# Low parts of streamed weights: a ScalarE negation and an adding DMA in place of a VectorE subtraction

## The chip, the cores and the metric

The kernel runs on one core of one Trainium2 chip. The metric is device time in microseconds (us) for one execution. A core has five engines with instruction queues of their own, each worked off in order: TensorE (PE in the profile, its weight loads PEld), VectorE (DVE), ScalarE (ACT), GpSimd (POOL) and SyncE (SP). DMAs are issued from the queues of SP, ACT and POOL, and 16 DMA engines move the data.

## The reference, cut to what matters

Two encoder layers on a sequence of 512 tokens of width 1024, all in float32. Nearly all the work is products of activations with weights that lie in device memory:

```
for l in range(DEPTH):                       # DEPTH = 2
    xn = rmsnorm(x, norm1_g[l])
    h = xn @ w_in[l]                         # projections of four token mixers
    ...                                      # the mixers a, b, c, d
    branch = jnp.einsum('bsnw,nwd->bsnd', ys, w_branch[l])
    gate = jax.nn.sigmoid(jnp.einsum('bsd,dne->bsne', xn, w_gate[l]))
    x = x + jnp.sum(gate * branch, axis=2) @ w_out[l]
    xn = rmsnorm(x, norm2_g[l])
    x = x + jnp.square(jax.nn.relu(xn @ w_mlp1[l])) @ w_mlp2[l]
return rmsnorm(x, final_norm_g)
```

## The kernel before

**High and low parts.** A product of float32 precision is made of three products of a rounded type (fp32r): each operand is cut into a high part (the value rounded to fp32r) and a low part (value minus high part), and TensorE adds high x high, high x low and low x high in PSUM. A weight block `raw` becomes `wh` (ScalarE, line 288, a cast) and `wl` (VectorE, line 289, `raw - wh`).

**Loads.** All products with weights stand in one list of items, the dense stream, and each item names its loads. A load is 512 KB: four blocks of 128 rows by 256 columns (`wl_a`; 512 runs of 1 KB in memory) or eight blocks by 128 columns (`wl_b`; 1024 runs of 512 B); in the chip's memory it is a tile of 128 partitions by 1024 elements. 276 loads come straight from a weight tensor and carry the key `"ap"` (40 of them `wl_b`). Two loads (`small`) are put together by several DMAs (`"custom"`). 98 loads (`"src"`) belong to the first MLP product: blocks `wq`, most of them sums and differences made by GpSimd at line 808. The change is in the 276.

**What a load goes through.** `emit_dma` (line 271) has SP load `raw` into tile `wr`, which has two buffers. `emit_split` makes `wh` and `wl` in `G['sp']` = 2 halves of 128x512 elements. Both tiles have three buffers, so the split of load i can begin only when TensorE has finished with load i - 3. (The last four loads of the second MLP product of each layer have buffers of their own, `twh` and `twl`.) TensorE then uses `wh` and `wl` in turns from its first matmuls on (lines 388 to 390, 402 to 404, 431 to 433).

**Order.** `Item.get(k)` is called when TensorE's matmuls of load i are about to be written down. It writes down the splits of all loads up to i + la, where `la` is 2 in the MLP and 1 elsewhere, then the preparing sums (`emit_pre`) and the DMAs up to i + 5. The mixers are generators. `drive` lets them run a step and then lets the dense stream run for so many estimated ns (`G`), so that dense matmuls stand between the steps of a mixer. The framework's scheduler may move an instruction ahead of another on the same engine, and it puts in all waits.

**Stages of a layer.** First come the norm and a front of projections and gates without a mixer beside them, then mixers a, d, b and c with projections, gates and branch products between their steps, then gates, branch products and `w_out` alone, the norm, and the MLP. In the MLP seven products `prod` of the first matrix (24 matmuls of 256 columns for each load) and four loads of the second (48 such matmuls each) take turns, seven times a layer; a last part (`tail_item`) closes it. After `prod` 6 the first load of the second matrix follows; this turn, from `m1` to `m2`, occurs 14 times in all.

Of the kernel before, what the change touches and what calls it, by code (L numbers as in the profile page):

```python
# [13 lines left out]
AF = mybir.ActivationFunctionType  # L14
ALU = mybir.AluOpType
AX = mybir.AxisListType

P = 128
# [14 lines left out]
G = dict(inv=1600, scan=1500, c=950, ss=300, kv=800, dr=1000, ds=1500, dh=1000, b1=900, b2=1100, b3=700, pd=8, ce=1100, hl=0, yp=4, pr=0, ps=0, b4=500, yn=1300, yw=1500, yt=1600, cl=3, sp=2, la=2, bl=(3, 5, 8), co=2500)  # L33
# [75 lines left out]
def encoder(ctx: ExitStack, tc: tile.TileContext, a: dict, out: bass.AP, dbg: dict = None):  # L109
    nc = tc.nc  # L110
    dbg = dbg or {}
    pe, dve, act, pool = nc.tensor, nc.vector, nc.scalar, nc.gpsimd
# [4 lines left out]
    sp = ctx.enter_context(tc.tile_pool(name="sp", bufs=8))  # L117
# [7 lines left out]
    def nm(s):  # L125
        cnt[0] += 1
        return f"{s}_{cnt[0]}"
# [23 lines left out]
    def f(ap):  # L151
        return ap.bitcast(F32)
# [80 lines left out]
    class Item:  # L233
# [6 lines left out]
        def get(self, k):  # L240
            i = self.i0 + k
            last = len(loads) - 1
            la = G['la'] if self.label[:2] in ("m1", "m2") else 1
            while ns_[0] <= min(i + la, last):
                stage(np_, ns_[0], emit_pre)
                emit_split(ns_[0])
                ns_[0] += 1
            stage(np_, min(i + 2 + la, last), emit_pre)
            stage(nd, min(i + 5, last), emit_dma)
            return wt.pop(i)  # L250

    def stage(ptr, upto, fn):
        while ptr[0] <= upto:
            if fn is emit_pre:
                stage(nd, ptr[0], emit_dma)
            fn(ptr[0])
            ptr[0] += 1
# [20 lines left out]
    def emit_split(i):  # L278
        w = loads[i]
        raw = w["src"]() if "src" in w else raws.pop(i)  # L280
        if "dest" in w:
            wh, wl = w["dest"]()
        else:
            wh = wp.tile([P, w["kt"], w["nc"]], F32R, tag="wh", name=nm("wh"))
            wl = wp.tile([P, w["kt"], w["nc"]], F32R, tag="wl", name=nm("wl"))
        n = w["kt"] // G["sp"]
        for k in range(0, w["kt"], n):
            act.copy(wh[:, k:k + n], raw[:, k:k + n])  # L288
            dve.tensor_tensor(wl[:, k:k + n], raw[:, k:k + n], f(wh[:, k:k + n]), op=ALU.subtract)  # L289
        wt[i] = (wh, wl)  # L290

# [1442 lines left out]
```

## Time and profile before

| | us |
|---|---|
| runs | 2342.53, 2341.07, 2341.0 |
| median | 2341.07 |
| the profiled execution, its own time | 2341.32 |
| its span, first to last instruction | 2339.3 |

The profile is of one execution. The 2.0 us between its span and its time lie around the instructions. A busy share is an average over all stages. What a change in one stage is worth is read from that stage and from the engine whose work ends last there. Matmuls are pipelined, so that the time of one (0.28 us for 256 columns) is longer than the step from one to the next.

### The profile page before, as it was taken

What the parts mean: (1) busy time and instruction counts of PE and PEld (TensorE: products, weight loads), DVE (VectorE), ACT (ScalarE), POOL (GpSimd) and SP (SyncE); (2) the same over time, 40 slices, a digit from 0 to 9 for tenths busy, and PEclk for the clock granted to TensorE, in tenths of its full rate; (3) what the DMA queues carried; (4) which work ended last, traced back from release to release, by engine and by line L of the source; (5) the groups of instructions that cost most, each with busy time, mean ns of one, the idle gap of its engine ahead of it and who ended that gap; (6) DMA issues with size and microseconds to landing.
All of it is one profiled execution on the core that took longest, in us unless ns stands there. A gap on an engine that the chain in (4) does not pass through costs nothing. (4 is left out here: it accounts for less than half of the span.)

```text
span 2339.3 us, 41459 instructions
## 1 busy us (share of the span) xinstructions
PE 2265.6 (97%) x16040; PEld 2027.1 (87%) x16040; DVE 1600.2 (68%) x2944; ACT 1236.9 (53%) x2827; POOL 749.8 (32%) x803
## 2 busy tenths in 40 slices
PE   7999999999999999999999999999999999999998
PEld 6879987878788989999987899878877889899998
DVE  5874547697886477677767745487877854867775
ACT  4565454765764264443445654367576633534443
POOL 1145452032332034443201545412313310434341
PEclk9999999999999999999999999999999999999999
DMA  6322131222122423233323111311322234233322
GB/s 153 99 46 64 50 92 59 64 91 82 51 71 82 162 71 123 87 109 109 111 75 91 55 55 60 96 54 55 100 73 64 64 115 137 88 95 109 100 82 91
DMA packets 234628, 200.80 MB, mean 86 GB/s; under 512 B 31680, under 2 KB 223552, under 8 KB 234432
## 3 DMA queue, kind: packets, MB, share of 16 engines
q1 hardware_dynamic: 231408, 193.08, 27.5%
q10 hardware_dynamic: 2304, 4.20, 0.5%
q8 instruction: 126, 2.06, 0.4%
q0 software_dynamic: 720, 0.89, 0.2%
q14 instruction: 70, 0.57, 0.1%
HBM read 190.24 MB, written 8.39 MB: 85 GB/s over the span
## 5 line engine op out<-in xcount | busy, mean ns | idle before, releaser
L289 DVE TENSOR_TENSOR wl<-wr,wh 128x512 fp32r<-128x512 f32 x540 | 405.3, 770 | 171.0 <-ACT wh L288 165.1
L288 ACT CAST wh<-wr 128x512 fp32r<-128x512 f32 x540 | 317.1, 621 | 220.4 <-PE pd L432 81.9
L431 PE MATMUL pd<-xh,wh 128*128 128x512 f32 (+1 forms) x768 | 309.1, 403 | 0.5 <-ACT xh L218 0.5
L432 PE MATMUL pd<-xl,wh 128*128 128x512 f32 (+1 forms) x768 | 298.4, 389 | 1.8 <-DVE xl L219 1.8
L433 PE MATMUL pd<-xh,wl 128*128 128x512 f32 (+1 forms) x768 | 298.4, 389 | 0.0
L389 PE MATMUL pd<-wl,hh 128*128 128x256 f32 x896 | 248.5, 277 | 0.0
L388 PE MATMUL pd<-wh,hh 128*128 128x256 f32 x896 | 248.0, 277 | 0.0
L390 PE MATMUL pd<-wh,hl 128*128 128x256 f32 x896 | 247.9, 277 | 0.0
L288 ACT CAST wh<-wq 128x512 fp32r<-128x512 f32 x196 | 115.2, 619 | 219.3 <-PE pd L390 92.8
L289 DVE TENSOR_TENSOR wl<-wq,wh 128x512 fp32r<-128x512 f32 x196 | 182.1, 963 | 13.3 <-ACT wh L288 13.2
L808 POOL TENSOR_TENSOR wq<-wq,wq 128x512 f32<-128x512 f32 x84 | 124.5, 1490 | 161.8 <-DVE wl L289 152.5
L433 PEld LDWEIGHTS pd<-xh,wl 128*128 128x128 f32 x768 | 146.0, 190 | 30.5
L432 PEld LDWEIGHTS pd<-xl,wh 128*128 128x128 f32 x768 | 146.7, 191 | 26.0 <-DVE xl L219 2.8
L388 PEld LDWEIGHTS pd<-wh,hh 128*128 128x128 f32 x896 | 168.2, 188 | 0.0
L390 PEld LDWEIGHTS pd<-wh,hl 128*128 128x128 f32 x896 | 168.2, 188 | 0.0
L389 PEld LDWEIGHTS pd<-wl,hh 128*128 128x128 f32 x896 | 168.1, 188 | 0.0
L431 PEld LDWEIGHTS pd<-xh,wh 128*128 128x128 f32 x768 | 146.2, 191 | 23.6 <-ACT xh L218 1.0
L676 DVE TENSOR_TENSOR x<-pd,x 128x512 f32<-128x512 f32 x124 | 85.2, 689 | 100.5 <-PE pd L390 100.4
L388 PE MATMUL pd<-wh,xh 128*128 128x256 f32 x512 | 151.0, 295 | 0.0
L389 PE MATMUL pd<-wl,xh 128*128 128x256 f32 x512 | 145.4, 284 | 0.0
L390 PE MATMUL pd<-wh,xl 128*128 128x256 f32 x512 | 145.0, 283 | 0.0
L1006 POOL TENSOR_TENSOR r<-r,r 128x512 f32<-128x512 f32 x26 | 36.5, 1402 | 300.7 <-PE pd L433 123.9
(393 smaller groups left out, 6631.6 us busy)
## 6 DMA issues: line engine op xcount, KB each, us to landing
wr<-in_w_in SPq DMA_DIRECT2D x92, 512.0 KB
wr<-in_w_mlp SPq DMA_DIRECT2D x72, 512.0 KB
wr<-in_w_gate SPq DMA_DIRECT2D x64, 512.0 KB
wq<-in_w_mlp SPq DMA_DIRECT2D x56, 512.0 KB
wr<-in_w_branch SPq DMA_DIRECT2D x32, 512.0 KB
wr<-in_w_out SPq DMA_DIRECT2D x16, 512.0 KB
x<-in_x SPq DMA_DIRECT2D x16, 256.0 KB
gsd<-gs ACTq DMA_DIRECT2D x16, 256.0 KB
```

What stands on the lines that cost most here:

```text
L288: act.copy(wh[:, k:k + n], raw[:, k:k + n])
L289: dve.tensor_tensor(wl[:, k:k + n], raw[:, k:k + n], f(wh[:, k:k + n]), op=ALU.subtract)
L388: mm(o, th, wh[:, k4, :], start=(kt == 0 and tt % 2 == 0), stop=False)
L389: mm(o, th, wl[:, k4, :], start=False, stop=False)
L390: mm(o, tl, wh[:, k4, :], start=False, stop=(kt == kts - 1 and tt % 2 == 1))
L431: mm(o, w1_, xh[kt][:, sl], start=(kt == 0 and hi_ == 0), stop=False)
L432: mm(o, w1_, xl[kt][:, sl], start=False, stop=False)
L433: mm(o, w2_, xh[kt][:, sl], start=False, stop=last)
L676: dve.tensor_tensor(d, bank.rearrange("p (t c) -> p t c", t=2), d, op=ALU.add)
L808: pool.tensor_tensor(d[:, k:k + 2], x[:, k:k + 2], y[:, k:k + 2], op=op)
L1006: pool.tensor_tensor(t, t, sh, op=ALU.add)
```

## The change

For loads with `"ap"` the cast is made in one piece. ScalarE then writes the negated high part into `wl`, and GpSimd issues a DMA that reads the weight block from memory a second time and adds it to `wl`. VectorE's subtraction is gone for these loads. `la` is 2 everywhere, and the memory set aside for descriptors of GpSimd's DMAs is doubled.

```diff
@@ -240,7 +240,7 @@
         def get(self, k):
             i = self.i0 + k
             last = len(loads) - 1
-            la = G['la'] if self.label[:2] in ("m1", "m2") else 1
+            la = G['la']
             while ns_[0] <= min(i + la, last):
@@ -283,9 +283,13 @@
-        n = w["kt"] // G["sp"]
+        n = w["kt"] // (1 if "ap" in w else G["sp"])
         for k in range(0, w["kt"], n):
             act.copy(wh[:, k:k + n], raw[:, k:k + n])
+            if "ap" in w:
+                act.activation(wl[:, k:k + n], f(wh[:, k:k + n]), AF.Copy, scale=-1.0)
+                pool.dma_start(wl[:, k:k + n], w["ap"].rearrange("(k p) c -> p k c", p=P)[:, k:k + n], accum_op=ALU.add)
+                continue
             dve.tensor_tensor(wl[:, k:k + n], raw[:, k:k + n], f(wh[:, k:k + n]), op=ALU.subtract)
         wt[i] = (wh, wl)
@@ -1719,7 +1723,7 @@
-    nc = bacc.Bacc("TRN2", target_bir_lowering=False, num_devices=1, dynamic_dma_scratch_size=4096)
+    nc = bacc.Bacc("TRN2", target_bir_lowering=False, num_devices=1, dynamic_dma_scratch_size=8192)
```

## Rows read from the trace of the kernel before

**Rows 1.** The page: span, and busy time of each engine.
```profile
span 2339.3 us, 41459 instructions
...
PE 2265.6 (97%) x16040; PEld 2027.1 (87%) x16040; DVE 1600.2 (68%) x2944; ACT 1236.9 (53%) x2827; POOL 749.8 (32%) x803
```

**Rows 2.** Stretches: us, busy PE, PEld, DVE, ACT, POOL, clock, DMA share, GB/s.
```profile
117.00:367.00 250.00, 245.11 (x2192) 214.63 (x2191) 137.02 (x226) 127.71 (x322) 120.93 (x150) 0.99 0.23 64
...
575.00:715.00 140.00, 133.65 (x677) 108.45 (x676) 115.62 (x358) 102.02 (x298) 45.30 (x49) 1.00 0.22 67
715.00:823.00 108.00, 108.00 (x642) 94.47 (x641) 51.75 (x94) 38.60 (x84) 15.64 (x13) 1.00 0.40 126
...
882.00:1148.00 266.00, 266.00 (x2306) 266.00 (x2305) 195.73 (x261) 117.22 (x207) 104.29 (x80) 1.00 0.33 101
```

**Rows 3.** Waits of PE: waited for, us in total, times, longest.
```profile
PE pm L483 <- DVE nj L468: 15.9, 9, 8.8
...
PE pm L833 <- DVE wl L289: 5.7, 2, 2.9
```

**Rows 4.** Timeline, turn from m1 to m2: cast, then TensorE's first matmul of that load.
```profile
2156.75 1.14 ACT L288 CAST wh<-wr 128x512 fp32r<-128x512 f32 x2 [1.63 <-PE pm L832]
...
2162.35 0.28 PE L388 MATMUL pd<-wh,hh 128*128 128x256 f32 x1
```

**Rows 5.** Timeline, gates alone: cast, then the first matmul of that load.
```profile
757.38 1.15 ACT L288 CAST wh<-wr 128x512 fp32r<-128x512 f32 x2 [1.62 <-PE pd L432]
...
768.54 0.39 PE L431 MATMUL pd<-xh,wh 128*128 128x512 f32 x1
```

**Rows 6.** Timeline, beside mixer a: cast, then the first matmul of that load.
```profile
249.20 1.23 ACT L288 CAST wh<-wr 128x512 fp32r<-128x512 f32 x2
...
271.98 0.28 PE L388 MATMUL pd<-wh,xh 128*128 128x256 f32 x1
```

**Rows 7.** Timeline, start of the MLP: cast of its second load, its first matmul.
```profile
831.54 1.14 ACT L288 CAST wh<-wr 128x512 fp32r<-128x512 f32 x2
...
835.96 0.28 PE L780 MATMUL pd<-xh,wh 128*128 128x256 f32 x1
```

**Rows 8.** Groups by line: busy us, mean ns | idle before, releasers.
```profile
L289 DVE TENSOR_TENSOR wl<-wr,wh 128x512 fp32r<-128x512 f32 x540 | 405.3, 770 | 171.0 <-ACT wh L288 165.1 <-PE pm L1152 4.3 <-PE pm L1614 0.2
L288 ACT CAST wh<-wr 128x512 fp32r<-128x512 f32 x540 | 317.1, 621 | 220.4 <-PE pd L432 81.9 <-PE pd L390 40.7 <-PE pm L832 22.0
...
L218 ACT CAST pth<-pm 128x128 fp32r<-128x128 f32 x160 | 40.8, 259 | 33.9 <-DVE ptl L219 24.5 <-PE pm L1604 9.4
```

**Rows 9.** Timeline: a 512 KB load issued by SP, the cast that waited for it.
```profile
2165.16 0.37 SPq L271 DMA_DIRECT2D wr<-in_w_mlp  x1
...
2168.65 1.15 ACT L288 CAST wh<-wr 128x512 fp32r<-128x512 f32 x2 [0.69 <-DMA wr<-in_w_mlp]
```

**Rows 10.** DMAs issued by POOL: size, us from issue to landing.
```profile
c_sgn<-in_sgn POOLq DMA_DIRECT2D x1, 448.0 KB, 7.0
c_negr<-in_neg POOLq DMA_DIRECT2D x1, 320.0 KB, 3.7
...
c_identr<-in_ident POOLq DMA_DIRECT2D x1, 64.0 KB, 3.7
...
c_identh<-in_ident POOLq DMA_DIRECT2D x1, 32.0 KB, 3.2
```

**Rows 11.** Timeline of POOL: one of these issues, 128 runs.
```profile
21.37 0.54 POOL L196 DMA_DIRECT2D c_negr<-in_neg  x1
```

**Rows 12.** SP's DMA queue: packets, MB, share of 16 engines.
```profile
q1 hardware_dynamic: 231408, 193.08, 27.5%
```

**Rows 13.** Stretches as in rows 2: a gap of PE, the stretch behind it, another gap.
```profile
863.70:866.70 3.00, 0.10 (x2) 0.03 (x1) 2.19 (x3) 1.38 (x3) 1.77 (x2) 1.00 0.00 0
867.27:870.68 3.41, 3.41 (x19) 3.41 (x18) 3.41 (x5) 0.00 (x0) 2.17 (x2) 0.50 0.00 0
...
628.00:629.90 1.90, 0.11 (x2) 0.04 (x1) 1.84 (x9) 1.13 (x4) 1.02 (x1) 1.00 0.20 62
```

## The prediction

> **What bounds the kernel now.** I read the busy shares first. TensorE is busy for 2265.6 of 2339.3 us, VectorE for 68%, ScalarE 53%, GpSimd 32% [rows 1]. Then the stretches: where no mixer runs, TensorE has no gap at all, in the gates and `w_out` (715 to 823) and in the MLP (882 to 1148); beside the mixers it loses 5 to 6 us in 250 or 140 us [rows 2]. So TensorE's order of work is the time, and a change of another engine counts only where it makes TensorE wait or ends a wait. TensorE's waits give what could be won: the longest is for the norm on VectorE (15.9 us), and the subtraction that the change touches appears with 5.7 us, both times for a `wq` block, which is not changed [rows 1, 3]. All idle time is 2339.3 - 2265.6 = 73.7 us.
>
> The next question is how early a load is ready, since the change lengthens its way. A cast begins when TensorE frees the third buffer (the releaser in the row). From the start of the cast to TensorE's first matmul of that load I find 5.60 us at the turn from `m1` to `m2` [rows 4], 11.16 us in gates alone [rows 5], 22.8 us beside mixer a [rows 6], and 4.4 us for the second load of the MLP [rows 7]. The first two are two loads' worth of matmuls, short at the turn because a `prod` has half as many. `la` = 2 can't lengthen them: three buffers set them, and the cast already starts when the buffer comes free.
>
> **Removed.** Two subtractions of 0.770 us for each of 276 loads [rows 8]: VectorE loses 425 us. They are done before TensorE needs them everywhere, so this alone gives nothing on TensorE's path except where a mixer's or norm's own VectorE step comes sooner. Of the 73.7 us idle I take 20 us as reachable in this way; bounds 0 and 25 us, a third of it.
>
> **Added on ScalarE.** A cast of 128x512 takes 621 ns and one of 128x128 259 ns [rows 8], 0.943 ns a column, so one of 128x1024 takes 621 + 512 x 0.943 = 1.10 us; the negation the same. A load costs ScalarE 2.21 us where it cost 1.24, in all +267 us, 53% to 64%. In the busiest mixer stretch, 575 to 715, with some 16 loads (one in 9 us), ScalarE goes from 73% to about 84%, VectorE from 83% to about 65%. What stands behind the negation on ScalarE, evacuations and mixer steps, waits 1 us more. I let this and the gain on VectorE cancel to +10 us, bounds -25 to +60.
>
> **Added on GpSimd and the DMA engines.** 276 issues and 276 x 512 KB. No row shows an adding DMA. Nearest below: a POOL DMA of 64 or 320 KB lands 3.7 us after its issue [rows 10]. Nearest above: one of 448 KB, which reads twice that and converts, behind four others, took 7.0 us [rows 10]. SP's 512 KB load took 3.5 us [rows 9]; the adding one has three streams in place of two and starts like a POOL DMA. A 512 KB load costs 27.5% x 2339.3 / (193.08 / 0.524) = 1.75 us of all 16 engines [rows 12]; a second read adds about that. I take 6.3 us from issue to landing, nearer to the 448 KB row, and keep 3.7 and 10. The issue itself is 0.54 us on POOL for 128 runs [rows 11]; a weight load has 512 or 1024. If each run costs, it is 2.2 or 4.3 us; I take 1 us inside the 6.3.
>
> The Trainium skill speaks here against the change: by "Collectives: The Full Stack" (The bandwidth ceiling) an add in the DMA path isn't dear itself but needs two source reads, which halved the measured rate. No run here shows it yet. By it the share of the DMA engines for an added load is 3.5 us, by a plain copy 1.75 us.
>
> **The way of a load, new:** cast 1.10 + negation 1.10 + hand-overs 0.2 + 6.3 = 8.7 us.
>
> - At the turn from `m1` to `m2`: 8.7 - 5.6 = 3.1 us late, 14 times, 43 us. The three loads behind it begin 2.8 to 5.4 us apart and TensorE spends 5.44 us on each (48 matmuls), so they are not late again as long as the way is under 10.9 us.
> - The clock: after a TensorE gap of 2.9 us the granted clock is 0.50, the level of 1.2 GHz, for 3.41 us; after one of 1.8 us it stays at 1.00 [rows 13]. Six such stretches are in the trace, each after a gap of 2.6 us or more. Each costs half its length, 1.7 us; 14 of them 24 us.
> - Second load of the MLP: 8.7 - 4.4 + 1.7 = 6 us, twice, 12 us.
> - Gates, `w_out` and the fronts alone, about 70 loads at 5.55 us: the way of 8.7 fits into 11.16. But the DMA engines, 0.40 busy there [rows 2], get 3.5 us more in each 5.55 us: 1.03. That is the limit; I take 0.3 us a load, 20 us (0 if the add costs a copy's share, 0.72).
> - Beside the mixers 8.7 us fit into 22.8 [rows 6], with a load about every 9 us at the least into some 16. POOL is 48% busy in 117 to 367 [rows 2], and an issue may stand behind a sum of 1.4 us that waits for the mixer; behind the issue wait the mixer's own sums. Nothing taken beyond the +10.
>
> Sum: 43 + 24 + 12 + 20 + 10 = 109 us. Against the profiled execution's own 2341.3 us, 0.25 us over the median, that is 2450 us. Ends: landing at 3.7 gives a way of 6.1 us, 7 us at the turns, 3 at the second load, -25 to 0 beside the mixers, 2326 to 2351; landing at 10 gives 12.4 us, so (6.8 + 1.7) x 14 = 119, 19 at the second loads, 70 x 0.65 = 46 where two loads' matmuls no longer cover it, 60 beside the mixers, 2585.
>
> **Rivals.**
>
> *Hidden, and VectorE's relief pays.* If the adding DMA lands within 3.2 us, as the 32 KB one did [rows 10], the way is 5.6 us and no turn is late; the relief of 20 us is left, 2321 us. The point is a landing of 3.2 us. Against it: 64 KB already took 3.7. By the Trainium skill, "DMA: Bandwidth & Descriptors" (Anatomy of one DMA), a POOL DMA takes about 2.0 us plus its bytes at 436 GB/s, an estimate of 3.2 us for 512 KB. The 64 KB row at 3.7 us is above that. 8%, and 12% that the landing is between this and 5 us (2346 to 2400 us).
>
> *The DMA engines become the bound.* If the add costs three copies' share, 5.25 us, gates and `w_out` want 2.2 + 5.25 = 7.5 us a load for 5.55 us of matmuls: 1.9 x 70 = 137 us. In the MLP, 0.33 + 4 x 5.25 / 41.6 = 0.83, the landings stretch to some 9.6 us and the way to 12: 113 us at the turns. With 20 at the other places, 2611 us. For it: the share of 1.03 above. 17%.
>
> *POOL writes each run.* 2.16 us for each of 236 loads and 4.3 us for 40: POOL +683 us, to 61%, in 117 to 367 to about 75%. The way becomes 10.3 us (12.5 for the 40): turns 90, second loads 20, 24 loads of the fronts at +0.65 16, gates 20, mixers' own sums delayed 40; 2527 us. 13%.
>
> *The change doesn't reach what bounds.* 98 of 376 loads keep their subtraction, and `la` acts on nothing that the buffers don't set; that is in the sum.
>
> **How the numbers follow.** A measurement tells about 0.2%, 5 us. Forecast near 2450 us (2400 to 2500): 50%. The range takes in the small landing, POOL's rival and the DMA bound and leaves out about 8% below and 10% above: 2350 to 2640 us. Faster 7% (the first rival, less a little), within 0.2% 5% (a landing near 3.7 with relief and stalls alike), slower 88%.
>
> **What would show it.** In the profile after: VectorE near 1180 us, ScalarE near 1500; TensorE waiting at line 388 or 389 for a POOL DMA of `wl` at each of 14 turns, 3 us, with a stretch at clock 0.50 behind it; no such waits beside the mixers; the DMA share near 1 in the gates. The adding DMA's row gives issue to landing: 6.3 right, 4 or 10 wrong by the terms above. Waits of TensorE for `wl` in the mixers, or mixer sums on POOL waiting for the issue, would make POOL's rival right.

## The result and the profile after

The changed kernel takes 2570.3 us (median of 4 runs, 2565.6 to 2573.6) against 2341.2 us in the runs beside it: ratio 1.098, 95% interval 1.096 to 1.099. It is slower, in the range that was given, but by 229 us where 109 were forecast. The profiled execution took 2565.6 us; its span is 224.5 us longer than that of [rows 1].

The page after: span and busy time by engine, the two DMA queues that carry the load, the median landings of the adding DMAs, and issues of them on GpSimd.

```profile
span 2563.8 us, 41353 instructions
...
PE 2325.7 (91%) x16040; PEld 2072.9 (81%) x16040; DVE 1263.2 (49%) x2392; ACT 1471.8 (57%) x2827; POOL 1076.9 (42%) x1079
...
q0 software_dynamic: 166928, 145.61, 39.2%
q1 hardware_dynamic: 231408, 193.08, 25.5%
...
L291 POOL DMA_DIRECT2D wl<-in_w_in x92 | 129.9, 1412 | 307.5 <-ACT wl L290 220.2
...
wl<-in_w_in POOLq DMA_DIRECT2D x92, 512.0 KB, 6.2
...
wl<-in_w_gate POOLq DMA_DIRECT2D x64, 512.0 KB, 6.1
```

VectorE is down by 337 us, ScalarE up by 235, GpSimd up by 327. TensorE has the same 16040 matmuls and is busy for 60 us more, since a part of them now runs at the low clock; the other 164 us are waits. GpSimd's queue q0 on the page before:

```profile
q0 software_dynamic: 720, 0.89, 0.2%
```

From 0.2% it went to 39.2%: (39.2% - 0.2%) x 2563.8 / 276 = 3.6 us of all 16 engines for each adding load.

Where TensorE waits now (waits of PE: waited for, us in total, times, longest):

```profile
PE pd L393 <- DMA wl<-in_w_mlp: 87.3, 16, 7.7
PE pm L487 <- DVE nj L472: 21.8, 7, 8.4
PE pd L408 <- DMA wl<-in_w_in: 15.2, 6, 5.8
PE pm L1371 <- DVE vb L1362: 10.9, 10, 2.8
```

The first line stands where [rows 3] had nothing: the low-part matmul of an `m2` load waits for its adding DMA, 14 turns and two more places. The second is the old wait for the norm.

The stretches of the first layer (columns as in [rows 2]; the same work as there, found by TensorE's loads): mixer a, mixer b's end, gates and `w_out`, MLP.

```profile
130.00:387.00 257.00, 243.51 (x2156) 212.25 (x2155) 106.15 (x170) 154.22 (x333) 146.78 (x191) 0.99 0.63 119
614.00:755.00 141.00, 135.03 (x684) 111.01 (x683) 98.56 (x319) 110.54 (x290) 62.21 (x64) 0.99 0.62 124
755.00:866.00 111.00, 107.08 (x609) 91.56 (x607) 24.13 (x55) 55.28 (x84) 36.70 (x31) 0.98 0.93 205
918.00:1262.00 344.00, 299.90 (x2431) 297.76 (x2430) 167.95 (x218) 151.66 (x227) 156.00 (x121) 0.93 0.55 125
```

The gates and `w_out` are where the DMA engines are fullest (0.93), and TensorE has lost only 3.9 us there. The MLP has a DMA share of 0.55 on the mean and has lost 44 us of TensorE's time to gaps, at a mean clock of 0.93.

To place the loss I took, for each of the 376 loads, the start of TensorE's first matmul of it after and before, and the growth of the difference over each part of the program. Later tables use the same parts, both layers together, in us. The border between the fronts and the mixers is soft: one load more or less moves 3 us. The start of the MLP begins here with the last load of `w_out`.

```
                       forecast   measured
turns m1 to m2, MLP          67      122.7
start of the MLP             12       23.3
fronts                       20       32.7
gates and w_out     (in the 20)       10.5
mixers                       10       35.4
sum                         109      224.6
```

One turn, seen closely (timeline of the fourth group in layer 0: ScalarE, GpSimd and TensorE):

```profile
1088.18 1.05 ACT L288 CAST wh<-wr 128x1024 fp32r<-128x1024 f32 x1 [1.64 <-PE pm L836]
1089.01 3.01 POOL L812 TENSOR_TENSOR wq<-wq,wq 128x512 f32<-128x512 f32 x2
1090.23 0.63 ACT L848 ACTIVATE c<-c 128x512 f32<-128x512 f32 x1 [1.00 <-DVE c L853]
1090.77 1.05 ACT L290 ACTIVATE wl<-wh 128x1024 fp32r<-128x1024 f32 x1
1092.17 1.31 POOL L291 DMA_DIRECT2D wl<-in_w_mlp  x1 [0.16 <-issue]
...
1093.78 0.63 PE L392 MATMUL pd<-wh,hh 128*128 128x256 f32 x4
...
1095.10 1.30 POOL L291 DMA_DIRECT2D wl<-in_w_mlp  x1 [0.55 <-ACT wl L290]
...
1098.03 1.30 POOL L291 DMA_DIRECT2D wl<-in_w_mlp  x1 [0.55 <-ACT wl L290]
...
1100.24 0.58 PE L393 MATMUL pd<-wl,hh 128*128 128x256 f32 x1 [5.84 <-DMA wl<-in_w_mlp]
```

TensorE reaches the load 5.60 us after its cast began, exactly the lead of [rows 4]. The negation begins 2.59 us after the cast, not 1.1: the square's relu stands between them and waits for VectorE. GpSimd finishes its two sums of `wq` only at 1092.02 and issues at 1092.17, 3.99 us after the cast. The DMA lands after 8.03 us. Over the 14 turns the medians are 3.99 us to the issue, 7.64 us to the landing, 11.63 us in all, against 8.7 in the forecast. The stretches of the same turn, same columns:

```profile
1094.41:1100.24 5.83, 0.00 (x0) 0.00 (x0) 1.99 (x3) 3.78 (x6) 4.73 (x5) 0.68 1.13 208
1100.24:1103.20 2.96, 2.96 (x14) 2.96 (x15) 0.00 (x0) 0.00 (x0) 0.17 (x1) 0.50 1.17 242
```

TensorE stands for 5.83 us, the granted clock falls to 0.50, its lower level, during the gap, and 14 matmuls after it run at that level. The DMA share is 1.13 to 1.17 (it adds up the packets' times, so it can pass 1): the second and third adding DMA, issued 2.9 us apart, run beside the first one.

### The profile page after: what moved, and what is told of

Its sections match the earlier page's. It is cut to its first block, busy times and chain, and to the rows that moved or that the text cites. A ratio compares the mean times of both kernels' runs of the same rounds, so it can differ in the third digit from the quotient of the medians.

```text
span 2563.8 us, 41353 instructions
## 1 busy us (share of the span) xinstructions
PE 2325.7 (91%) x16040; PEld 2072.9 (81%) x16040; DVE 1263.2 (49%) x2392; ACT 1471.8 (57%) x2827; POOL 1076.9 (42%) x1079
## 3 DMA queue, kind: packets, MB, share of 16 engines
q0 software_dynamic: 166928, 145.61, 39.2%
q1 hardware_dynamic: 231408, 193.08, 25.5%
## 4 chain that ended last, share of the span: by engine, by line
PE 55%; DMA 11%; ACT 11%; DVE 8%; POOL 7%; issue 6%; SPq 1%; POOLq 0%; DVEq 0%; ACTq 0%
PE pd L393 6%; PE pd L394 6%; PE pd L392 6%; DMA wl<-in_w_mlp 5%; PE pd L435 5%; PE pd L437 5%; PE pd L436 5%; ACT wh L288 2%; PE pd L408 2%; PE pd L406 2%; PE pd L407 2%; DMA wl<-in_w_in 2%; POOL wq L812 2%; PE pm L836 1%; PE pm L835 1%
## 5 line engine op out<-in xcount | busy, mean ns | idle before, releaser
L288 ACT CAST wh<-wr 128x1024 fp32r<-128x1024 f32 (+1 forms) x272 | 283.8, 1044 | 339.6 <-PE pd L394 162.9
L393 PE MATMUL pd<-wl,hh 128*128 128x256 f32 x896 | 263.2, 296 | 87.3 <-DMA wl<-in_w_mlp 87.3
L290 ACT ACTIVATE wl<-wh 128x1024 fp32r<-128x1024 f32 x268 | 283.9, 1059 | 4.0
L394 PE MATMUL pd<-wh,hl 128*128 128x256 f32 x896 | 259.7, 292 | 0.0
L291 POOL DMA_DIRECT2D wl<-in_w_in x92 | 129.9, 1412 | 307.5 <-ACT wl L290 220.2
L392 PE MATMUL pd<-wh,hh 128*128 128x256 f32 x896 | 254.1, 290 | 2.6 <-ACT wh L288 2.6
L393 PEld LDWEIGHTS pd<-wl,hh 128*128 128x128 f32 x896 | 182.5, 204 | 90.6 <-DMA wl<-in_w_mlp 90.5
L394 PEld LDWEIGHTS pd<-wh,hl 128*128 128x128 f32 x896 | 182.4, 204 | 0.0
L392 PEld LDWEIGHTS pd<-wh,hh 128*128 128x128 f32 x896 | 178.5, 202 | 3.0 <-ACT wh L288 3.0
L291 POOL DMA_DIRECT2D wl<-in_w_gate x64 | 83.2, 1300 | 223.1 <-ACT wl L290 177.0
```

The costliest lines, as they stand in the source:

```text
L290: act.activation(wl[:, k:k + n], f(wh[:, k:k + n]), AF.Copy, scale=-1.0)
L291: pool.dma_start(wl[:, k:k + n], w["ap"].rearrange("(k p) c -> p k c", p=P)[:, k:k + n], accum_op=ALU.add)
L392: mm(o, th, wh[:, k4, :], start=(kt == 0 and tt % 2 == 0), stop=False)
L393: mm(o, th, wl[:, k4, :], start=False, stop=False)
L394: mm(o, tl, wh[:, k4, :], start=False, stop=(kt == kts - 1 and tt % 2 == 1))
```

## The experiments

The theory after the result: a load costs what its way (cast, negation, issue, landing) exceeds its lead (cast to TensorE's first matmul), plus the low clock behind the gap; at the turns the landing is long because three adding DMAs run together. Rivals: the look-ahead or ScalarE's new work; GpSimd's place in the chain; a fixed cost per load through the engines.

**What is not the cause: look-ahead, ScalarE, VectorE.**

```diff
 # e1_la_only: the kernel before with
-            la = G['la'] if self.label[:2] in ("m1", "m2") else 1
+            la = G['la']
 # e8_no_add: the changed kernel without
-                pool.dma_start(wl[:, k:k + n], ..., accum_op=ALU.add)
```

> The kernel before with only the look-ahead of 2 for every load; the subtraction stays on VectorE. Theory (the way of an adding load is what costs): three buffers already set when a cast can begin, so 2341 us within 5. Rival (the earlier casts and subtractions stand ahead of the mixers' own steps, and this is the mixers' part of the loss): 2360 to 2380 us.

> The changed kernel without the 276 adding DMAs: the low part stays the negated high part, so the product of the low part is left out in what it means, not in its work. ScalarE's negation and the look-ahead stay. Theory (the landing is the late part of the way): the way at the turns falls from 11.6 to 3.6 us, under the lead of 5.6, no turn is late, and VectorE's relief shows: 2320 to 2345 us. Rival (ScalarE's extra 292 us is what delays the mixers): the mixers' 40 us stay, 2370 to 2390 us.

Measured: look-ahead alone 2352.0 us, ratio 1.005 (1.004 to 1.007); without the adding DMAs 2346.0 us, 1.002 (1.001 to 1.003). The look-ahead costs 11 us, against both expectations: more than my 5, less than the rival's 20; by parts 9.6 us of it are in the mixers. With the negation on ScalarE as well and 382 us less on VectorE (1217.9 us busy) the time is 6 us below that; what each of the two is worth was not separated. All but some 6 us of the loss comes with the DMA.

**GpSimd in the chain.** Three kernels put something else in the adding DMA's place.

```diff
 # in place of pool.dma_start(wl[:, k:k + n], ..., accum_op=ALU.add)
 # e14_pool_touch
+                pool.tensor_tensor(wl[:, k, 0:2], f(wl[:, k, 0:2]), raw[:, k, 0:2], op=ALU.add)
 # e16_pool_busy
+                pool.tensor_tensor(wl[:, 0:2], f(wl[:, 0:2]), raw[:, 0:2], op=ALU.add)
 # e11_small_add
+                pool.dma_start(wl[:, 0, 0:64], w["ap"][0:P, 0:64], accum_op=ALU.add)
```

> The changed kernel with each adding DMA cut from 512 KB to 32 KB: the low part is right in 64 columns of one of its four blocks alone, the rest stays the negated high part. What waits for what stays, the bytes go. Theory (half of a landing and more is the transfer, 3.6 us of all 16 engines): landing at 4 to 4.5 us, the way at the turns 3.6 + 4.3 = 7.9, late by 2.3 us, mostly without a fall of the clock: 14 x 2.3 = 32, 5 to 15 elsewhere over the 2346 us without the DMA: 2375 to 2395 us. Rival (GpSimd's place in the chain costs by itself: its sums stand behind an issue that waits for the negation): the mixers' 30 us stay, 2400 to 2440 us.

> The changed kernel with each adding DMA replaced by a sum of two columns on GpSimd that reads and writes the low part, so the rest of the low part stays the negated high part: GpSimd still waits in its order for ScalarE's negation, and TensorE for GpSimd, but nothing is issued and nothing has to land. The run with 32 KB DMAs kept 34 to 37 us of loss in the two mixer stretches though it landed in 2.6 us. Theory (that loss is GpSimd's order: the mixers' own sums stand behind an instruction that waits for the negation): the mixers' 30 to 37 us stay and the turns are on time, 2372 to 2385 us. Rival (it is the DMA itself, its issue of 0.9 us and its landing): 2345 to 2356 us, as without the DMA.

> The changed kernel with each adding DMA replaced by a sum of 512 columns on GpSimd, 1.3 us, as long as the issue of the adding DMA; so the second half of the low part stays the negated high part. No DMA. Theory (the mixers lose by GpSimd's time for the issue): the mixers lose 20 to 35 us over the 2349 us of the run with a sum of two columns, 2368 to 2385 us. Rival (it is the DMA that slows them, by the engines or by what its issue does to VectorE): 2346 to 2356 us.

Measured: 2424.2 us with 32 KB, ratio 1.035 (1.033 to 1.036); 2348.7 us with a sum of two columns, 1.003; 2393.5 us with a sum of 512 columns, 1.023 (1.021 to 1.024). By parts:

```
                     changed  32 KB  512 columns  2 columns
turns, MLP             122.7   30.5          3.9        2.4
start of the MLP        23.3    7.6          0.8        0.3
fronts                  32.7    7.8         14.6        2.0
gates and w_out         10.5    2.4          3.1        1.0
mixers                  35.4   37.4         29.5        2.1
```

The GpSimd lines of the three: first the issue of 32 KB (duration ns min/median/max) and its landing in us, then the two sums (busy us, mean ns | idle before).

```profile
L291 POOL DMA_DIRECT2D wl<-in_w_in x92: 849/876/1134, 38.9 to 1804.8; - x92
...
wl<-in_w_in POOLq DMA_DIRECT2D x92, 32.0 KB, 2.6
```
```profile
L291 POOL TENSOR_TENSOR wl<-wl,wr 128x512 fp32r<-128x512 f32 (+1 forms) x268 | 332.6, 1241 | 711.2 <-ACT wl L290 586.1 <-issue 86.2 <-ACT dn L1455 15.9
```
```profile
L291 POOL TENSOR_TENSOR wl<-wl,wr 128x2 fp32r<-128x2 f32 x268 | 60.6, 226 | 836.7 <-ACT wl L290 678.8 <-issue 119.2 <-ACT dn L1455 15.9
```

My theory for the two-column sum fell: GpSimd stands idle for the negation 679 us in all, and the run is only 2.6 us slower than the one without the DMA. So the wait for the negation is not what costs the mixers. They lose when the instruction in the DMA's place is longer: 2.1 us with the sum of 0.23 us, 29.5 with the sum of 1.24, 37.4 with the small issue of 0.88, 35.4 with the issue of 512 KB of 1.3 to 1.4. The losses don't follow the durations, so GpSimd's time alone doesn't account for them.

The long sum is not a clean stand-in for an issue either, since VectorE gets slower beside it. Two VectorE instructions of one kind in that run, the second beside GpSimd's sum:

```profile
909.58 0.69 DVE L851 TENSOR_TENSOR hl<-pp,hh 128x512 fp32r<-128x512 f32 x1 [1.59 <-POOL pp L850]
...
911.86 1.30 POOL L291 TENSOR_TENSOR wl<-wl,wr 128x512 fp32r<-128x512 f32 x1
911.93 1.78 DVE L851 TENSOR_TENSOR hl<-pp,hh 128x512 fp32r<-128x512 f32 x1 [1.06 <-POOL pp L850]
```

An issue doesn't do this: in the changed kernel 149 VectorE instructions ran beside an issue for more than 0.4 us and beside nothing else of GpSimd, and none took over 0.05 us longer than the shortest of its kind. So the 27 us that the long sum costs the mixers (29.5 - 2.1) can't be put down to the issue as they stand, nor can the 15 us in the fronts, which took this run past its expectation (2368 to 2385). What is shown is that the mixers' loss comes with the DMA or an instruction as long on GpSimd; that TensorE loses it by GpSimd's time is argued. The 32 KB run missed its expectation (2375 to 2395) by the mixers' 37 us and lies in its rival's range, though not by the wait that the rival named.

**How much is the bytes, how much the addition.**

```diff
 # e4_copy
-                pool.dma_start(wl[:, k:k + n], ..., accum_op=ALU.add)
+                pool.dma_start(wl[:, k:k + n], ...)
```

> The changed kernel with a plain DMA of the weights into the low part where the adding one was; the addition is left out, the negation and the issue on GpSimd stay. Packets of SP's plain queue take half the time of the adding ones (46 to 54 against 102 to 109 ns for 1 KB). Theory (the time of the transfer on the DMA engines is about half of the landing, and three of them overlap at a turn): the landing falls from 6.1 to about 4.3 us alone and from 7.6 to 5.5 at the turns, 2 us less lateness and 0.5 to 1 less at the low clock for each of 14 turns, some 15 us elsewhere: 2505 to 2530 us. Rival (the landing is a fixed cost of GpSimd's queue, whatever is moved): 2560 to 2575 us.

Measured: 2458.5 us, ratio 1.051 (1.049 to 1.053), 112 us back, well over what I expected. Landing and queue (as on the page):

```profile
q0 software_dynamic: 166928, 145.61, 27.4%
...
wl<-in_w_in POOLq DMA_DIRECT2D x92, 512.0 KB, 4.5
```

(27.4% - 0.2%) x 2454.7 / 276 = 2.4 us of 16 engines, against 3.6 with the addition. At the turns the first landing takes 4.05 us (median of 14) against 7.64, the way is 8.38, late by 2.8, and the turns cost 55.3 us in place of 122.7, 4 us each in place of 8.8. The mixers lose 22 us in place of 35; the plain DMA's issue takes GpSimd 0.74 to 0.81 us (medians by tensor). I had reckoned with a landing of 5.5 us at the turns; at two thirds of the engines' time the three DMAs hardly hold each other up.

**The turns alone, and the burst.**

```diff
 # e2_m2_sub: the changed kernel, adding DMA only where
+                d["add"] = label[:3] != "m2_"
 # e12_first_only
+                d["add"] = label[:3] != "m2_" or label[5] == "0"
```

> The changed kernel, but the 56 loads of m2 keep the subtraction on VectorE. Theory: the loss sits at the 14 turns from m1 to m2, where a step of TensorE comes about 8.0 us later, so 14 x 8.0 = 112 us come back and 2570 becomes 2455 to 2465 us. Rival (each adding load costs about the same wherever it stands, through the DMA engines or the queues): 56 of 276 loads give back 0.20 x 229 = 46 us, 2524 us.

> The changed kernel, but of the four loads of m2 that follow each turn only the first goes by the adding DMA; the other three keep the subtraction. Theory (the first landing takes 7.6 us at a turn and 6.1 alone because two more adding DMAs follow it 2.9 us apart and share the 16 engines): alone it lands in 6.1, the way is 3.99 + 6.1 = 10.1 us, late by 4.5 instead of 6.0, and the low clock shrinks by as much: 6 us for each of 14 turns over the 2451 us of the run in which no m2 load adds, 2525 to 2545 us. Rival (the landing at the turns is long by the raw loads of SP that run beside it, or by something else that stands there anyway): 8 us a turn as in the changed kernel, 2555 to 2570 us.

Measured: 2451.2 us for the first, ratio 1.047 (1.046 to 1.049), so 119 us belong to the 56 loads of `m2`, a fifth of the loads and half of the loss. With the adding DMA for the first load of each turn alone 2532.3 us, 1.082 (1.080 to 1.084), inside the expectation. The same turn in that kernel:

```profile
1078.20 1.05 ACT L291 CAST wh<-wr 128x1024 fp32r<-128x1024 f32 x1 [1.64 <-PE pm L839]
...
1082.18 1.31 POOL L294 DMA_DIRECT2D wl<-in_w_mlp  x1 [0.16 <-issue]
...
1088.04 0.39 PE L396 MATMUL pd<-wl,hh 128*128 128x256 f32 x1 [2.35 <-DMA wl<-in_w_mlp]
```

Issue 3.98 us after the cast as ever, landing 5.81 us later (1087.99) in place of 8.03; over the 14 turns the median is 5.81 against 7.64. So the 1.8 us by which a landing at a turn exceeds one that stands alone are the following adding DMAs, and SP's raw loads, which run here as well, are not needed for it.

**Shortening the way, lengthening the lead.**

```diff
 # e5_neg_dve
-                act.activation(wl[:, k:k + n], f(wh[:, k:k + n]), AF.Copy, scale=-1.0)
+                dve.tensor_scalar(wl[:, k:k + n], f(wh[:, k:k + n]), -1.0, 0.0, op0=ALU.mult, op1=ALU.add)
 # e6_buf4 (e9_before_buf4: the same on the kernel before, with its subtraction)
-NAR = 26
+NAR = 25
+            la = 3 if self.label[:2] in ("m1", "m2") else G['la']
+            wh = wp.tile(..., tag="wh", name=nm("wh"), bufs=4)
+            wl = wp.tile(..., tag="wl", name=nm("wl"), bufs=4)
```

> The changed kernel with the negation on VectorE in place of ScalarE. At the turns the negation stood 2.59 us behind the start of the cast, 1.5 more than the cast lasts, because the square's relu stood between them on ScalarE and waited for VectorE. Theory (this queueing on ScalarE is a term of the lateness): the way at the turns gets 1 to 1.5 us shorter, 14 to 25 us for the 14 turns with the low clock, a few at the fronts: 2535 to 2560 us. Rival (only the landing counts, or VectorE's queue holds the negation up as long): 2563 to 2580 us.

> The changed kernel with four buffers of the high and low part where it had three, a look-ahead of 3 in the MLP, and 25 tiles of the small arena where it had 26. Theory (a lead of two products, 5.6 us, against a way of 11.6 us makes the turns late): the lead grows by one product, 2.8 us, the lateness falls from 6.0 to some 3.2 us and with it a part of the low clock, 3 to 4.5 us for each of 14 turns: 2505 to 2530 us. Rival (the cast stands behind other work of ScalarE, or the raw tile comes too late, so that a free buffer changes nothing): 2560 to 2580 us.

> The kernel before with the same buffers, the same look-ahead and the same smaller arena, the subtraction on VectorE: the control for the run with four buffers. Both theories: 2352 us within 6, as with the look-ahead alone; if more, the difference is the arena's and is taken off the other run.

Measured: negation on VectorE 2568.3 us, ratio 1.097 (1.095 to 1.098): nothing gained. Its turn shows why:

```profile
1087.86 1.05 ACT L288 CAST wh<-wr 128x1024 fp32r<-128x1024 f32 x1 [1.36 <-PE pm L836]
...
1090.39 0.68 DVE L290 TENSOR_SCALAR wl<-wh 128x1024 fp32r<-128x1024 f32 x1
...
1091.28 1.04 POOL L850 TENSOR_TENSOR c<-c 128x512 f32<-128x512 f32 x1 [0.86 <-ACT hh L849]
1092.26 1.30 POOL L291 DMA_DIRECT2D wl<-in_w_mlp  x1
```

The negation takes 0.68 us and ends 3.21 us after the start of the cast, but GpSimd's own square stands before the issue and waits for ScalarE; it issues after 4.40 us. Here the wait that was taken from one queue came back in the next.

Four buffers: 2493.1 us, ratio 1.064 (1.063 to 1.066), less than I expected (2505 to 2530); the control 2354.5 us, 1.005. The loss over the control is 138.6 us, where the changed kernel lost 218.3 over its own (the look-ahead alone). The start of the MLP has nothing left of its 23.3 us; the turns keep 92 of 122.7. The lead at a turn grows from 5.60 to 8.45 us, as expected, but the lateness falls only by 2.1 us, from 6.07 to 3.93 (medians of 14), since the landing is longer beside more adding DMAs: the first lands after 9.05 us (median of 14), the later ones after 10 to 13.

**The rule, tried where it should cost nothing.**

```diff
 # the kernel before, adding DMA only where
 # e13_slack
+                d["add"] = (label[:3] == "m2_" and label[5] in "23") or label[:3] in ("gc1", "gc2", "gc3", "mc1", "mc2", "mc3")
 # e17_gates_only
+                d["add"] = label[:3] in ("gc1", "gc2", "gc3", "mc1", "mc2")
```

> The kernel before, look-ahead as it was, with the adding DMA only for 46 loads whose lead is longer than the way: the third and fourth load of m2 behind each turn (28) and the loads of the gates and branches of mixer c, column blocks 1 to 3, that run alone (18). Theory (an adding load costs TensorE nothing where the way of 8.7 to 10 us fits into the lead, and VectorE's relief is worth nothing either): 2341 us within 5. Rival (each adding load costs something by the DMA engines or by GpSimd, 0.8 us as the mean over all 276): 2370 to 2385 us.

> The kernel before, look-ahead as it was, with the adding DMA for 16 loads alone: the gates of mixer c, column blocks 1 to 3, and its branches 1 and 2, whose casts in the profile before stand 10.7 to 12.7 us ahead of their matmuls. Theory (a way of 8.5 to 9 us inside that lead costs nothing): 2341 us within 4. Rival (0.8 us a load, the mean over all 276): 2354 us.

The first missed by far: 2422.4 us, ratio 1.035 (1.034 to 1.037). By parts 71.9 us are at the turns and 9.3 us at `w_out`. I had not read the lead of the third load of `m2` but taken it for long. The kernel before has it: cast and the first matmul of that load.

```profile
1011.05 0.61 ACT L288 CAST wh<-wr 128x512 fp32r<-128x512 f32 x1
```
```profile
1018.04 0.28 PE L388 MATMUL pd<-wh,hh 128*128 128x256 f32 x1
```

6.99 us. The adding load's way was 10.7 us there. In the changed kernel this lead did not show: TensorE stands for the first load, and the third has some 18 us. At `w_out` the last branch load had a lead of 11.08 us and yet came late, because its landing took 11.7 us. SP reads `x` again at that moment (timeline of the first kernel); that this reading is the reason was not tested by itself.

```profile
770.42 2.89 SPq L182 DMA_DIRECT2D x<-in_x  x6
...
771.74 1.28 POOL L294 DMA_DIRECT2D wl<-in_w_branch  x1
...
783.50 0.50 PE L440 MATMUL pd<-yh,wl 128*128 128x512 f32 x1 [3.35 <-DMA wl<-in_w_branch]
```

With the loads of `m2` and the last branch load left out the second kernel takes 2341.0 us, ratio 1.000 (0.999 to 1.001): 16 adding loads with leads of 10.7 us and more cost nothing, with the DMA engines at 0.67 in that stretch (715 to 823):

```profile
715.00:823.00 108.00, 107.88 (x642) 94.06 (x640) 39.63 (x77) 44.93 (x82) 24.57 (x20) 1.00 0.67 166
```

They gain nothing either, so no mix of the two kernels that I tried beats the kernel before.

## Why the prediction was right and wrong

Right: TensorE's order of work is the time, and VectorE's relief is worth next to nothing on it (without the DMAs VectorE has 382 us less to do, and the time is 5.6 us above that of the kernel before). The change makes loads late at the turns, in the place and by the wait that was named (`m2`'s low part for GpSimd's DMA, 14 times). Forecast landing 6.3 us, measured 6.1 to 6.2 (medians for `w_in` and `w_gate`); the 6.3 was a choice between rows of 3.7 and 7.0 us, so that it came so close is in part luck. Forecast cast and negation 1.10 us each, measured 1.05 and 1.06. In the gates the way is 9.0 us (median; 8.2 at the least), near the 8.7 forecast.

An adding load takes 3.6 us of all 16 engines, a plain copy through the same queue 2.4. By the Trainium skill ("Collectives: The Full Stack", The bandwidth ceiling) an add needs two source reads; 3.5 us was the estimate from that. The agreement is luck in part, since the estimate doubled the 1.75 us of SP's queue: within GpSimd's queue the add costs half as much again, not twice. By the Trainium skill's "DMA: Bandwidth & Descriptors" (Anatomy of one DMA) the landing was an estimate of 3.2 us; the plain copy took 4.5 and the adding one 6.2, so that rival fell.

VectorE lost 337 us where 425 were forecast. The 425 add up single durations that overlap (the group's busy time in [rows 8] is 405.3), and in the changed kernel other VectorE instructions got longer (the last list). The range held the time, but by other terms: its upper end, 2585 us, had 46 us for the gates, `w_out` and the fronts alone and 60 for the mixers.

Wrong, the terms of the sum, largest first:

- **"At the turn from `m1` to `m2`: 8.7 - 5.6 = 3.1 us late."** The lead of 5.6 was right, the way was 11.63 us: late by 6.0, 14 x 6.0 = 84 in place of 43 us. The way was put together from durations of a load alone. At the turn the issue comes 3.99 us after the cast, where a load in a quiet place has it after 2.5: the negation stands behind the square's relu, and where that is taken away the issue stands behind GpSimd's own square. And the landing is 7.64 instead of 6.3 us, since three adding DMAs at 3.6 us of all engines each follow 2.9 us apart. That demand could be worked out beforehand (3.5 us in the 2.8 between the casts); I compared it with the gates' 5.55 us instead.
- **The clock**, 14 x 1.7 = 24 us: right in kind, a third too small. A turn makes TensorE 8.4 us later on the mean, of which the gap is 5.9; the other 2.5 us, 34 us in all, are matmuls at the low clock. The granted clock is at 0.50 for 6.8 us at 11 of the 14 turns, where [rows 13] has 3.41, and part of that lies in the gap.
- **"Nothing taken beyond the +10" in the mixers**: 35.4 us. The issue takes 1.3 to 1.4 us of GpSimd, where I put 1 us into the landing and nothing in front of the mixers' own work. The runs show that the loss comes with such an instruction on GpSimd (37.4 us with 32 KB, 29.5 with a long sum, 2.1 with a short one); how it reaches TensorE is open. The look-ahead, costed at nothing, takes 9.6 us by itself; with VectorE's relief and the short sum 2.1 are left.
- **"Gates, `w_out` and the fronts alone": 0.3 us a load for the DMA engines, 20 us.** The gates lost nothing at a share of 0.93 (and nothing in the run with 16 loads), so that step is wrong; 8 of the 10.5 us are one load a layer, the last branch load, which runs beside the reading of `x`. The fronts lost 32.7 us for another reason: many of their leads are not the 11.16 us of [rows 5]. The front load that costs most, in the kernel before:

```profile
35.11 1.14 ACT L288 CAST wh<-wr 128x512 fp32r<-128x512 f32 x2 [2.86 <-DMA wr<-in_w_in]
```
```profile
37.59 0.39 PE L402 MATMUL pd<-xh,wh 128*128 128x512 f32 x1
```

  2.48 us, and the way of this load was 9.6 us after the change; TensorE lost 9.5 us there. Most others in the fronts have 5 to 11 us. I carried one stretch's lead over to another.
- **Second load of the MLP**, 12 us: the start of the MLP lost 23.3. The second load itself cost 16.7 of them: its lead was right, but its way was 12.7 and 11.1 us in the two layers, with landings of 9.7 and 8.1. The other 6.6 stand at the last load of `w_out`, whose lead of 6.6 us I had not read, against ways of 10.1 and 8.4. Four buffers take nearly all of it away.

Of the rivals, "the DMA engines become the bound" had the mechanism of the turns (a way of 12 us) under a wrong condition: the share is 3.6 and not 5.25 us, and the gates, where it was to cost 137 us, lost nothing. "POOL writes each run" put 40 us on the mixers, near the 35.4, but by an issue of 2.2 to 4.3 us, where 1.3 and 1.6 were measured.

What stays open: by what path an issue on GpSimd costs the mixers their 35 us, and how the fronts' loss divides between landings, leads and GpSimd. Whether the order on ScalarE and GpSimd could be mended together, so that cast, negation and issue follow each other at the turn, was not tried.

## What to carry to other kernels

Put the way of a new transfer together at the place where it is shortest of time, from what stands in front of it on every queue that it crosses and from the transfers that follow within its own landing; a mean share of the DMA engines says nothing of a burst (0.93 cost next to nothing in the gates, a mean of 0.55 went with 44 us of gaps in the MLP). Read the lead of each kind of load in its own stretch, and don't carry one over. A DMA issued by GpSimd is also an instruction of GpSimd, 1.3 us here: count it where other work stands in that queue. And a stand-in for one term of a change can bring a cost of its own, as the long sum did with VectorE.

## What the runs showed of the hardware beyond that

- An adding DMA of 512 KB took 3.6 us of 16 engines, a plain one through the same queue 2.4, one through SP's queue 25.5% x 2563.8 / (193.08 / 0.524) = 1.8. Median landings for `w_in`: 6.2 us adding, 4.5 plain; 2.6 us for an adding one of 32 KB, faster than the 3.2 us of the 32 KB one in [rows 10].
- Issuing an adding DMA took GpSimd 0.88 us for 32 KB in 128 runs, 1.3 for 512 KB in 512 runs, 1.57 in 1024 runs, far from 2.2 or 4.3. A plain one of 512 KB took 0.74 to 0.81.
- The negation of 128x1024 took 1.06 us on ScalarE and, in the turn shown, 0.68 us on VectorE.
- A VectorE sum that GpSimd feeds got longer (duration ns min/median/max of one line, before and after), and TensorE waits for it 10.9 us in all where it waited 0.7. Its longest, 3.25 us, ran beside GpSimd's sums and copies from start to end; in the kernel before none took over 1.09 us. That this is a path by which an issue costs the mixers is likely by the trace but was not tested.

```profile
L1358 DVE TENSOR_TENSOR vb<-vb,t x12: 681/732/1090, 243.5 to 1520.2; 128x512 f32<-128x512 f32 x12
```
```profile
L1362 DVE TENSOR_TENSOR vb<-vb,t x12: 682/1697/3250, 266.4 to 1661.3; 128x512 f32<-128x512 f32 x12
```
